# Where the weight sums of a seven-product feed forward are made: DVE adds in place instead of accumulating DMAs, and the relu stores issued by SP

## The chip, the cores and the metric

The kernel runs on 1 core of one Trainium2 chip. The metric is the device time of one execution, in microseconds (us). Before the change the median of 3 runs is 1975.8 us (1973.03 to 1976.18).

## The reference

The program is one decoder block on 1024 tokens of width 1024: an S5 state-space mixer beside dilated window attention, cross attention to 256 memory tokens, and a squared-relu feed forward, each closed by a layer norm. The change touches the feed forward alone:

```python
D_FF = 4 * D_MODEL            # 1024 -> 4096 -> 1024, all float32
ff = jnp.square(jax.nn.relu(h @ w_ff1[l] + b_ff1[l])) @ w_ff2[l] + b_ff2[l]
h = layer_norm(DEEPNORM_ALPHA * h + ff, ln3_g[l], ln3_b[l])
```

## The kernel before

Both matrix products of the feed forward are cut into 2x2 quadrants and multiplied with seven products instead of eight (the Winograd form of Strassen's scheme). The seven weight operands of a block come from its four quadrants 11, 12, 21, 22: "1" is 11, "2" is 21, "3" is 22, "5" is 11+12, "7" is 12+22, "6" is 11+12+22 and "4" is the sum of all four. Each operand is split into a high part and a rest (ACT makes the high part by a cast, DVE subtracts it), and a product is three rounds of float32r matmuls over four pieces of depth: 12 matmuls of 128x512.

*First product* (here: stage one; 16 blocks j of two times 128 hidden columns). `operand` (L1468) makes one operand: the cast on L1472, the subtraction on L1473, and then whatever the raw quadrants need next. The raw quadrants of two blocks (even and odd j) lie in buffers X, Y, Z, V; blocks of even j have theirs in the tiles `wraw`, those of odd j in free corners of the tile `hn` and in `sg`. Before the change, the sums are made by DMA: `add_in` (L1457) issues a DMA from the queue of POOL that adds its source to what lies in the destination. In every block X takes 12 on top of 11, Z takes 12 on top of 22, V is built as 11+12+22, and Y takes V. The plain loads for block j+2 go out on the queue of SP as soon as a buffer has been read for the last time. Six pairs of split buffers `whi`/`wlo`, each for two operands, hold the operands ahead of TensorE: a pair is filled when the pair six before it has been multiplied (`Stream`, L114; `slot` and `pump` issue the work).

The results of the seven products are combined by `f1_evac`, which DVE runs from PSUM: after "2" one addition (L1589), after "6" the five operations L1593, L1594, L397, L1599 and L1603, after "4" one (L1607). ACT then applies relu (L1572) and square (L1573). Four operations of POOL (L1609 to L1614) make the sums of the activations that the second product needs. All seven results of a block are stored to HBM, into `f_dr` (L1584): numbers 1, 2 and 4 by ACT's queue, 5, 6, 7 and 3 by SP's. Every engine and queue takes its instructions in the order in which the program wrote them down; nothing reorders them.

*Second product* (stage two; 4 blocks c of 1024 hidden rows, 7 products each, 4 token groups t per product). Its stationary operands are read back from `f_dr` through the same stream: SP loads (L145), ACT casts (L158), DVE subtracts (L159). Its weight quadrants are 1 MB each; `f2_weights` makes an operand two products ahead (cast L1544, subtraction L1545), and again `add_in` makes the sums from HBM. The first block's raw weights are loaded from POOL's queue (L1531), behind POOL's work of stage one. The residual input, saved in `h2_dr`, is brought back by four 1 MB loads on POOL's queue (L1809) at the start of stage two, and DVE adds products to it (L397, L1754).

The functions that the diff touches, and what calls them:

Of the kernel before, what the change touches and what calls it, by code (L numbers as in the profile page):

```python
# [58 lines left out]
def block_kernel(ctx, tc, I, out, dbg=None):  # L59
# [128 lines left out]
    W = Stream()  # L188
# [1271 lines left out]
    def f1_begin():  # L1460
        a, b = (win.tile([128, 1024], FT, name="wraw", tag="wraw", bufs=2) for _ in range(2))
        row = rows.tile([128, D], FT, name="row2", tag="row2", bufs=1)
        raws[0] = [half(a, 0), half(a, 1), half(b, 0), half(b, 1)]
        raws[1] = [half(row, 0), half(row, 1)]
        load(raws[0], 0, "11", "21", "22", "11")
        load(raws[1], 1, "11", "21")


    def operand(j, q, h, l):
        X, Y, Z, V = raws[j % 2] if len(raws[j % 2]) == 4 else raws[j % 2] + [None, None]  # L1470
        src = {"1": X, "2": Y, "3": Z, "4": Y, "5": X, "6": V, "7": Z}[q]
        act.copy(h, src)  # L1472
        dve.tensor_sub(l, src, h.bitcast(FT))  # L1473
        nxt = raws[(j + 1) % 2]
        if j == 0 and q in "12":
            add_in(V, w1(j, "12" if q == "1" else "22"))
        at = "57" if j == 1 else "15"
        if 0 < j < 15 and q in at:
            add_in(nxt[3], w1(j + 1, "12" if q == at[0] else "22"))
        if q == "1" and j != 1:  # L1480
            add_in(X, w1(j, "12"))
        elif q == "3":
            add_in(Z, w1(j, "12"))
# [10 lines left out]
        if j == 0 and q == "3":  # L1494
            add_in(Y, V)

# [17 lines left out]
    t_free = []  # L1514
    w2slot = []
    w2 = {}
# [10 lines left out]

    def w2_load(c, n, e=sp):
        if c < 4:
            w2[c, n] = w2slot.pop(0)  # L1530
            e.dma_start(w2[c, n], w2_src(c, n))  # L1531

    T2 = {}

    def f2_weights(n):
        if n >= len(f2_made):
            return
        c, q = f2_made[n]
        h, l = T2[c, q] = t_free.pop(0)
        X, Y, Z = (w2.get((c, i)) for i in ("11", "21", "22"))  # L1540
        if q == "6":
            add_in(Y, X)
        src = {"1": X, "2": Y, "3": Z, "4": Y, "5": X, "6": X, "7": Z}[q]
        act.copy(h, src)  # L1544
        dve.tensor_sub(l, src, h.bitcast(FT))  # L1545
        if q == "1":
            add_in(X, w2_src(c, "12"))
        elif q == "5":
            add_in(X, w2_src(c, "22"))
        elif q == "3":  # L1550
            add_in(Z, w2_src(c, "12"))
        elif q in "674":
            w2slot.append({"6": X, "7": Z, "4": Y}[q])
            if q != "4":
                w2_load(c + 1, "21" if q == "6" else "22")

# [22 lines left out]
    def f1_evac(j, q, p):  # L1579
# [102 lines left out]
    for n, (j, q) in enumerate(f1_seq):  # L1682
        p = bank()
        f1_product(j, q, p)
        f1_evac(j, q, p)
        if n == 1:
            W.cap = 10 ** 9
        slot()
        if j == 15:
            if q == "5":  # L1690
                wr = [actp.tile([128, 4, SEQ], FT, name="w2raw", tag=n) for n in ("acth0", "actl0")]
                w2slot += [a[:, :, 512 * i:512 * i + 512] for a in wr for i in range(2)]
# [229 lines left out]
```

## Time and profile before

| | |
|---|---|
| median of 3 runs | 1975.8 us |
| the profiled execution: its time, its span | 1979.96 us, 1978.2 us |
| TensorE busy / mean granted clock | 1832.2 us (93%) / 0.968 |
| DVE, ACT, POOL busy | 1188.8 (60%), 704.0 (36%), 760.4 (38%) us |
| moved by DMA | 273.43 MB, of it 50.86 MB on POOL's queue |
| stage one | about 1282 to 1596 us of the span |
| stage two | about 1596 to 1950 us, then 28 us of layer norm and stores |

A busy TensorE says little here, since a matmul that waits counts as idle only where nothing runs. Stage one holds 103 products after the first four half products, and stage two 112, each of 12 matmuls, so the time of a matmul in a stretch without waits, set against the time that the stretch took, tells what waiting costs. Two other things are to be read from such a page: which engine a waiting instruction names as its releaser, and who released that one. Here a chain of DVE and ACT, which wait for each other in turn, stands behind TensorE.

### The profile page before, as it was taken

The page shows a single profiled execution, that of the slowest core. Times are in us where ns is not written, and L with a number is a line of the kernel's source. Part 1 is how long each engine was busy: PE and PEld are TensorE (multiplying, and loading weights), DVE is VectorE, ACT ScalarE, POOL GpSimd, SP SyncE. Part 2 cuts the span into 40 slices and gives each one's busy share as a digit, 9 for nine tenths or more (in the row PEclk, how much of TensorE's full clock was granted, in tenths as well). Part 3 has the DMA queues.
Part 4 walks back from the last instruction along what each step waited for, and adds up shares of the span by engine and source line. Part 5 has one row for each costly group of instructions (what it writes and reads, how often), then busy time and mean ns, then how long its engine had stood idle before and what let it go on. Part 6 is the DMA issues. An engine that isn't in the chain of part 4 may idle for free. (4 is left out here: it accounts for less than half of the span.)

```text
span 1978.2 us, 24975 instructions
## 1 busy us (share of the span) xinstructions
PE 1832.2 (93%) x9112; PEld 1567.8 (79%) x9112; DVE 1188.8 (60%) x1994; ACT 704.0 (36%) x1176; POOL 760.4 (38%) x859
## 2 busy tenths in 40 slices
PE   7899999999999989999999999779999975999993
PEld 7798788899999977888887878658777754888872
DVE  6527736766665765344575466754555534765798
ACT  4333333332332435222124322434455443432421
POOL 3305696555556245222061023445455341001142
PEclk9999999999999999999999999899999987999997
DMA  6545561120211243424411133477778668889742
GB/s 253 179 119 193 184 195 44 57 73 25 86 34 35 83 138 102 136 90 137 177 47 43 54 115 103 108 190 197 193 209 216 183 198 245 247 207 208 221 119 85
DMA packets 138634, 273.43 MB, mean 138 GB/s; under 512 B 24720, under 2 KB 44304, under 8 KB 138512
## 3 DMA queue, kind: packets, MB, share of 16 engines
q1 hardware_dynamic: 100992, 195.28, 29.8%
q0 software_dynamic: 24560, 50.86, 13.8%
q10 hardware_dynamic: 12960, 25.70, 3.5%
q8 instruction: 72, 1.18, 0.2%
q14 instruction: 50, 0.41, 0.1%
HBM read 195.15 MB, written 68.26 MB: 133 GB/s over the span
## 5 line engine op out<-in xcount | busy, mean ns | idle before, releaser
L159 DVE TENSOR_TENSOR wlo<-wraw,whi 128x1024 fp32r<-128x1024 f32 (+1 forms) x171 | 217.6, 1279 | 224.5 <-ACT whi L158 223.8
L158 ACT CAST whi<-wraw 128x1024 fp32r<-128x1024 f32 (+1 forms) x171 | 170.7, 999 | 335.1 <-DMA wraw<-f_dr 159.7
L100 PE MATMUL mm<-whi,acth 128*128 128x512 f32 (+1 forms) x704 | 282.2, 401 | 0.0
L102 PE MATMUL mm<-whi,actl 128*128 128x512 f32 (+1 forms) x704 | 271.1, 385 | 0.0
L101 PE MATMUL mm<-wlo,acth 128*128 128x512 f32 (+1 forms) x704 | 270.9, 385 | 0.0
L100 PE MATMUL mm<-acth,whi 128*128 128x512 f32 (+1 forms) x640 | 248.5, 388 | 21.7 <-DVE hn L1593 8.4
L102 PE MATMUL mm<-acth,wlo 128*128 128x512 f32 (+1 forms) x640 | 245.7, 384 | 2.8 <-DVE wlo L159 2.5
L101 PE MATMUL mm<-actl,whi 128*128 128x512 f32 (+1 forms) x640 | 245.4, 383 | 0.3 <-DVE actl L279 0.3
L102 PEld LDWEIGHTS mm<-whi,actl 128*128 128x128 f32 x704 | 168.6, 239 | 15.4
L101 PEld LDWEIGHTS mm<-wlo,acth 128*128 128x128 f32 x704 | 169.1, 240 | 14.2
L100 PEld LDWEIGHTS mm<-whi,acth 128*128 128x128 f32 x704 | 168.1, 239 | 15.4
L100 PEld LDWEIGHTS mm<-acth,whi 128*128 128x128 f32 x640 | 124.1, 194 | 46.1 <-issue 14.6
L102 PEld LDWEIGHTS mm<-acth,wlo 128*128 128x128 f32 x640 | 123.4, 193 | 26.9 <-DVE wlo L159 3.0
L101 PEld LDWEIGHTS mm<-actl,whi 128*128 128x128 f32 x640 | 123.9, 194 | 22.1 <-DVE actl L279 0.5
L1473 DVE TENSOR_TENSOR wlo<-wraw,whi 128x512 fp32r<-128x512 f32 x56 | 53.2, 975 | 92.6 <-ACT whi L1472 92.6
L100 PE MATMUL ax<-acth,whi 128*128 128x512 f32 x232 | 93.7, 404 | 15.0 <-DVE hn L1593 10.5
L246 POOL TENSOR_TENSOR rs<-rs 128x2 f32<-128x2 f32 x30 | 18.4, 614 | 221.7 <-DVE rs L243 220.1
L101 PE MATMUL ax<-actl,whi 128*128 128x512 f32 x232 | 92.5, 399 | 3.2 <-DVE actl L1545 3.2
L102 PE MATMUL ax<-acth,wlo 128*128 128x512 f32 x232 | 92.5, 399 | 3.0 <-DVE wlo L159 3.0
L1458 POOL DMA_DIRECT2D w2raw<-in_wff_dram x12 | 14.6, 1216 | 201.5 <-DVE pl L1545 112.8
L1572 ACT ACTIVATE hn<-hn,cols 128x512 f32<-128x512 f32 x64 | 46.5, 727 | 117.3 <-DVE hn L397 52.2
L100 PE MATMUL ax<-ph,whi 128*128 128x512 f32 x164 | 65.3, 398 | 11.0 <-ACT ph L1544 11.0
(434 smaller groups left out, 4329.0 us busy)
## 6 DMA issues: line engine op xcount, KB each, us to landing
wraw<-f_dr SPq DMA_DIRECT2D x56, 512.0 KB
w2raw<-in_wff_dram POOLq DMA_DIRECT2D x15, 1024.0 KB, 10.5
f_dr<-hn SPq DMA_DIRECT2D x56, 256.0 KB
f_dr<-hn ACTq DMA_DIRECT2D x48, 256.0 KB
w2raw<-in_wff_dram SPq DMA_DIRECT2D x9, 1024.0 KB
wraw<-in_wg_dram SPq DMA_DIRECT2D x16, 512.0 KB
gl<-g_dr SPq DMA_DIRECT2D x32, 256.0 KB
wraw<-b_dr SPq DMA_DIRECT2D x16, 512.0 KB
```

Source lines behind the costliest of these rows:

```text
L100: pe.matmul(o, lhsT=lh, rhs=rh, start=first, stop=False)
L101: pe.matmul(o, lhsT=lh, rhs=rl, start=False, stop=False)
L102: pe.matmul(o, lhsT=ll, rhs=rh, start=False, stop=last)
L158: act.copy(h[:, :n], r[:, :n])
L159: dve.tensor_sub(l[:, :n], r[:, :n], h[:, :n].bitcast(FT))
L246: e.tensor_mul(t, z, z)
L1458: pool.dma_start(dst, src, accum_op=OP.add)
L1473: dve.tensor_sub(l, src, h.bitcast(FT))
L1572: act.activation(x, x, AF.Relu, bias=cols[:, COL_F1 + b:COL_F1 + b + 1], scale=1.0)
```

## The change

Stage one: the four quadrants are loaded plainly (V now takes 12) and DVE makes the sums in the buffers, right behind the subtraction that last needed the old content. Stage two: DVE makes 12+22 and 11+12+22; 11+12 (from block 1 on) and the sum of all four remain accumulating DMAs, but from one buffer on the chip to another. All seven stores of a block go out on SP's queue. The cap that held the filling of operands back in the first blocks is lifted earlier. The next block's quadrant 11 is loaded after operand "3" and not with product "1", the first block's 12 is loaded along with 21 and 11, and the gains of the last layer norm are loaded two products later.

```diff
@@ f1_begin
-        load(raws[0], 0, "11", "21", "22", "11")
+        load(raws[0], 0, "11", "21", "22", "12")
@@ operand
+        if (j, q) == (1, "5"):
+            dve.tensor_add(X, X, V)
+            dve.tensor_add(V, V, Z)
+            dve.tensor_add(Z, Z, X)
+        src = {"1": X, "2": Y, "3": Z, "4": Y, "5": X, "6": Z, "7": V}[q]
         act.copy(h, src)
         dve.tensor_sub(l, src, h.bitcast(FT))
-        nxt = raws[(j + 1) % 2]
-        if j == 0 and q in "12":
-            add_in(V, w1(j, "12" if q == "1" else "22"))
-        at = "57" if j == 1 else "15"
-        if 0 < j < 15 and q in at:
-            add_in(nxt[3], w1(j + 1, "12" if q == at[0] else "22"))
         if q == "1" and j != 1:
-            add_in(X, w1(j, "12"))
+            dve.tensor_add(X, X, V)
         elif q == "3":
-            add_in(Z, w1(j, "12"))
-        elif q == "2" and j > 1:
-            add_in(Y, V)
+            if j != 1:
+                dve.tensor_add(V, V, Z)
+                dve.tensor_add(Z, Z, X)
         elif q == "5":
             load([X], j + 2, "11")
         elif q == "6":
-            load([V], j + 2, "11")
+            dve.tensor_add(Y, Y, Z)
+            load([Z], j + 2, "22")
         elif q == "7":
-            load([Z], j + 2, "22")
+            load([V], j + 2, "12")
@@ f2_weights
-        if q == "6":
-            add_in(Y, X)
-        src = {"1": X, "2": Y, "3": Z, "4": Y, "5": X, "6": X, "7": Z}[q]
+        src = {"1": X, "2": Y, "3": Z, "4": Y, "5": X, "6": Z, "7": V}[q]
         act.copy(h, src)
         dve.tensor_sub(l, src, h.bitcast(FT))
-        if q == "1":
-            add_in(X, w2_src(c, "12"))
-        elif q == "5":
-            add_in(X, w2_src(c, "22"))
+        if n == 0:
+            dve.tensor_add(X, X, V)
+        elif q == "1":
+            add_in(X, V)
         elif q == "3":
-            add_in(Z, w2_src(c, "12"))
+            dve.tensor_add(V, V, Z)
+            dve.tensor_add(Z, Z, X)
+            add_in(Y, Z)
+            w2_load(c + 1, "11", X)
...
@@ f1_evac
-            (act if n in (1, 2, 4) else sp).dma_start(f_dr[n - 1, :, j, :], x)
+            sp.dma_start(f_dr[n - 1, :, j, :], x)
@@ first blocks of stage one
-    load(raws[1][3:], 1, "11")
-    add_in(raws[1][0], w1(1, "12"))
-    add_in(raws[1][3], w1(1, "12"))
-    add_in(raws[1][3], w1(1, "22"))
+    load(raws[1][3:], 1, "12")
...
-    add_in(raws[1][1], raws[1][3])
-    W.cap = W_FF + 6
+    W.cap = 10 ** 9
@@ end of stage one (j == 15, after product "5")
-                w2_load(0, "21", pool)
-                w2_load(0, "11", pool)
+                for i in (1, 0, 3):
+                    w2_load(0, ("11", "21", "22", "12")[i], w2slot[i], pool)
...
-    add_in(w2[0, "11"], w2_src(0, "12"))
-    w2_load(0, "22", pool)
+    w2_load(0, "22", w2slot[2], pool)
@@ stage two, loop over products
-                if (c, q) == (3, "1"):
+                if n == 23:
-                if q == "1" and c < 3:
-                    w2_load(c + 1, "11")
```

Lines of the changed kernel that stand in the rows below: L1477 is the subtraction of `operand`, L1479, L1482, L1483 and L1487 are the new additions, L1588 to L1606 are the operations of `f1_evac` (before: L1589 to L1607), L1583 is the store, L1527 the load of a quadrant of stage two.

On DVE, from the evacuation of product "2" of a block in stage one to the one after the next product "6", in the kernel before:

```order
L1589 TENSOR_TENSOR hn<-hn,ax 128x512
L1473 TENSOR_TENSOR wlo<-wraw,whi 128x512 x2
L1593 TENSOR_TENSOR hn<-mm,hn 128x512
L1594 TENSOR_TENSOR hn<-ax,hn 128x512
L397 SCALAR_TENSOR_TENSOR hn<-hn,mm 128x512
L1599 TENSOR_TENSOR hn<-hn,mm 128x512
L1603 TENSOR_TENSOR hn<-hn,mm 128x512
L1473 TENSOR_TENSOR wlo<-wraw,whi 128x512 x2
```

The same stretch in the changed kernel:

```order
L1588 TENSOR_TENSOR hn<-hn,ax 128x512
L1477 TENSOR_TENSOR wlo<-wraw,whi 128x512
L1479 TENSOR_TENSOR wraw<-wraw 128x512
L1477 TENSOR_TENSOR wlo<-wraw,whi 128x512
L1482 TENSOR_TENSOR wraw<-wraw 128x512
L1483 TENSOR_TENSOR wraw<-wraw 128x512
L1592 TENSOR_TENSOR hn<-mm,hn 128x512
L1593 TENSOR_TENSOR hn<-ax,hn 128x512
L397 SCALAR_TENSOR_TENSOR hn<-hn,mm 128x512
L1598 TENSOR_TENSOR hn<-hn,mm 128x512
L1602 TENSOR_TENSOR hn<-hn,mm 128x512
L1477 TENSOR_TENSOR wlo<-wraw,whi 128x512 x2
```

Three additions now stand in the queue ahead of the evacuation of product "6"; the order of the rest is the same.

On POOL, from the end of stage one into stage two, in the kernel before (L1614 is the last of the four sums of a block, L1458 an accumulating DMA, L1531 a weight load, L1809 a load of the residual):

```order
L1614 TENSOR_TENSOR sg<-hn 128x512
L1531 DMA w2raw<-in_wff_dram 128x4x512 x2
L1609 TENSOR_TENSOR hn<-hn 128x512
L1610 TENSOR_TENSOR hn<-hn 128x512
L1613 TENSOR_TENSOR hn<-hn 128x512
L1614 TENSOR_TENSOR hn<-hn 128x512
L1458 DMA w2raw<-in_wff_dram 128x4x512
L1531 DMA w2raw<-in_wff_dram 128x4x512
L1809 DMA hn<-h_dr 128x4x512 x2
L1458 DMA w2raw<-in_wff_dram 128x4x512
L1809 DMA hn<-h_dr 128x4x512
```

And in the changed kernel:

```order
L1613 TENSOR_TENSOR sg<-hn 128x512
L1527 DMA w2raw<-in_wff_dram 128x4x512 x3
L1608 TENSOR_TENSOR hn<-hn 128x512
L1609 TENSOR_TENSOR hn<-hn 128x512
L1612 TENSOR_TENSOR hn<-hn 128x512
L1613 TENSOR_TENSOR hn<-hn 128x512
L1527 DMA w2raw<-in_wff_dram 128x4x512
L1799 DMA hn<-h_dr 128x4x512 x3
L1458 DMA w2raw<-w2raw 128x4x512
L1799 DMA hn<-h_dr 128x4x512
```

The first accumulating DMA has become a plain load ahead of the last block's sums, and the third load of the residual no longer stands behind an accumulating DMA.

On SP, from the last stores of block 14 on, in the kernel before:

```order
L1584 DMA f_dr<-sg 128x512
L145 DMA wraw<-f_dr 128x1024 x3
L1584 DMA f_dr<-hn 128x512 x4
L145 DMA wraw<-f_dr 128x1024
L1531 DMA w2raw<-in_wff_dram 128x4x512
L145 DMA wraw<-f_dr 128x1024 x6
```

And in the changed kernel:

```order
L1583 DMA f_dr<-sg 128x512
L145 DMA wraw<-f_dr 128x1024
L1583 DMA f_dr<-hn 128x512
L145 DMA wraw<-f_dr 128x1024 x2
L1583 DMA f_dr<-hn 128x512 x6
L145 DMA wraw<-f_dr 128x1024 x7
L1527 DMA w2raw<-in_wff_dram 128x4x512 x2
```

The 1 MB load between the first and the second read-back after the stores has moved behind seven of them.

## Rows read from the trace of the kernel before

**Rows 1.** Stretches: span, busy PE, PEld, DVE, ACT, POOL, then PEclk, DMA share, GB/s.

```profile
1398.00:1560.00 162.00, 155.81 (x673) 127.56 (x674) 86.91 (x114) 79.42 (x128) 84.65 (x75) 0.98 0.79 203
1597.00:1668.00 71.00, 40.16 (x144) 30.64 (x144) 28.87 (x26) 23.35 (x24) 17.43 (x15) 0.79 0.74 234
1668.00:1895.00 227.00, 226.07 (x995) 186.84 (x994) 162.22 (x172) 84.22 (x66) 28.28 (x23) 1.00 0.88 225
```

**Rows 2.** Waits of PE, stage one, then 1596 to 1700 (us, times, longest).

```profile
PE ax L100 <- DVE hn L1593: 10.5, 6, 4.1
PE mm L100 <- DVE hn L1593: 9.9, 2, 8.4
...
PE ax L100 <- ACT ph L1544: 11.0, 1, 11.0
PE ax L101 <- DVE pl L1545: 10.6, 2, 7.4
```

**Rows 3.** DVE in order of time: start, us, work, idle before and its releaser.

```profile
1439.27 0.68 DVE L1593 TENSOR_TENSOR hn<-ax,hn 128x512 f32<-128x512 f32 x1
...
1447.97 1.74 DVE L1473 TENSOR_TENSOR wlo<-hn,whi 128x512 fp32r<-128x512 f32 x1 [4.64 <-ACT whi L1472]
...
1456.86 1.29 DVE L1473 TENSOR_TENSOR wlo<-wraw,whi 128x512 fp32r<-128x512 f32 x2 [2.53 <-ACT whi L1472]
...
1467.43 0.69 DVE L1473 TENSOR_TENSOR wlo<-wraw,whi 128x512 fp32r<-128x512 f32 x1 [2.21 <-ACT whi L1472]
...
1476.90 0.69 DVE L1473 TENSOR_TENSOR wlo<-wraw,whi 128x512 fp32r<-128x512 f32 x1 [2.54 <-ACT whi L1472]
...
1479.32 0.68 DVE L1593 TENSOR_TENSOR hn<-ax,hn 128x512 f32<-128x512 f32 x1
```

**Rows 4.** ACT in the same cycle.

```profile
1443.24 0.73 ACT L1572 ACTIVATE hn<-hn,cols 128x512 f32<-128x512 f32 x1 [0.40 <-ACT hn L1573]
...
1447.31 0.62 ACT L1472 CAST whi<-hn 128x512 fp32r<-128x512 f32 x1 [0.89 <-DMA hn<-in_wff_dram]
...
1466.78 0.63 ACT L1472 CAST whi<-wraw 128x512 fp32r<-128x512 f32 x1 [2.28 <-DMA wraw<-in_wff_dram]
```

**Rows 5.** DVE: an in-place subtraction alone; three subtractions beside POOL's sums.

```profile
1260.82 0.69 DVE L1384 TENSOR_TENSOR hn<-sg,hn 128x512 f32<-128x512 f32 x1
...
1566.81 4.78 DVE L1473 TENSOR_TENSOR wlo<-hn,whi 128x512 fp32r<-128x512 f32 x3 [3.64 <-ACT whi L1472]
```

**Rows 6.** ACT in the first blocks of stage one.

```profile
1307.03 0.62 ACT L1472 CAST whi<-wraw 128x512 fp32r<-128x512 f32 x1 [4.57 <-DMA wraw<-in_wff_dram]
...
1328.29 0.62 ACT L1472 CAST whi<-hn 128x512 fp32r<-128x512 f32 x1 [7.66 <-DMA hn<-in_wff_dram]
```

**Rows 7.** ACT, DVE, POOL and SP at the start of stage two, in this order.

```profile
1626.83 1.05 ACT L158 CAST whi<-wraw 128x1024 fp32r<-128x1024 f32 x1 [9.01 <-DMA wraw<-f_dr]
...
1638.86 1.05 ACT L158 CAST whi<-wraw 128x1024 fp32r<-128x1024 f32 x1 [10.49 <-DMA wraw<-f_dr]
1639.81 1.90 ACT L1544 CAST ph<-w2raw 128x2048 fp32r<-128x2048 f32 x1
...
1662.71 0.69 DVE L397 SCALAR_TENSOR_TENSOR hn<-hn,ax 128x512 f32<-128x512 f32 x1 [7.75 <-DMA hn<-h_dr]
1663.31 2.29 DVE L1545 TENSOR_TENSOR pl<-w2raw,ph 128x2048 fp32r<-128x2048 f32 x1
...
1621.70 1.24 POOL L1458 DMA_DIRECT2D w2raw<-in_wff_dram  x1
...
1645.95 1.24 POOL L1458 DMA_DIRECT2D w2raw<-in_wff_dram  x1 [18.95 <-DVE pl L1545]
1646.73 1.23 POOL L1809 DMA_DIRECT2D hn<-h_dr  x1
...
1622.20 0.38 SPq L145 DMA_DIRECT2D wraw<-f_dr  x1
1622.68 0.64 SPq L1531 DMA_DIRECT2D w2raw<-in_wff_dram  x1
```

More of the change, by code (lines that the diff above doesn't have):

```diff
@@ L1463, in f1_begin @@
         raws[0] = [half(a, 0), half(a, 1), half(b, 0), half(b, 1)]
-        raws[1] = [half(row, 0), half(row, 1)]
-        load(raws[0], 0, "11", "21", "22", "11")
+        raws[1] = [half(row, 0), half(row, 1), None, None]
+        load(raws[0], 0, "11", "21", "22", "12")
         load(raws[1], 1, "11", "21")
     def operand(j, q, h, l):
-        X, Y, Z, V = raws[j % 2] if len(raws[j % 2]) == 4 else raws[j % 2] + [None, None]
-        src = {"1": X, "2": Y, "3": Z, "4": Y, "5": X, "6": V, "7": Z}[q]
+        X, Y, Z, V = raws[j % 2]
+        if (j, q) == (1, "5"):
[3 more added lines that the diff above has]
+        src = {"1": X, "2": Y, "3": Z, "4": Y, "5": X, "6": Z, "7": V}[q]
         act.copy(h, src)
         dve.tensor_sub(l, src, h.bitcast(FT))
-        nxt = raws[(j + 1) % 2]
-        if j == 0 and q in "12":
-            add_in(V, w1(j, "12" if q == "1" else "22"))
-        at = "57" if j == 1 else "15"
-        if 0 < j < 15 and q in at:
-            add_in(nxt[3], w1(j + 1, "12" if q == at[0] else "22"))
         if q == "1" and j != 1:
-            add_in(X, w1(j, "12"))
+            dve.tensor_add(X, X, V)
         elif q == "3":
-            add_in(Z, w1(j, "12"))
-        elif q == "2" and j > 1:
-            add_in(Y, V)
+            if j != 1:
+                dve.tensor_add(V, V, Z)
+                dve.tensor_add(Z, Z, X)
         elif q == "5":
@@ L1488, in operand @@
         elif q == "6":
-            load([V], j + 2, "11")
+            dve.tensor_add(Y, Y, Z)
+            load([Z], j + 2, "22")
         elif q == "7":
-            load([Z], j + 2, "22")
+            load([V], j + 2, "12")
         elif q == "4":
             load([Y], j + 2, "21")
-        if j == 0 and q == "3":
-            add_in(Y, V)
     f1_order = "1325764"
@@ L1514, in block_kernel @@
     t_free = []
-    w2slot = []
     w2 = {}
@@ L1526, in w2_src, with w2_load @@
         return I["wff2"][c, ("11", "12", "21", "22").index(n)].rearrange("p (j c) -> p j c", j=4)
-    def w2_load(c, n, e=sp):
+    def w2_load(c, n, dst, e=sp):
         if c < 4:
-            w2[c, n] = w2slot.pop(0)
-            e.dma_start(w2[c, n], w2_src(c, n))
+            w2[c, n] = dst
+            e.dma_start(dst, w2_src(c, n))
     T2 = {}
@@ L1539, in f2_weights @@
         h, l = T2[c, q] = t_free.pop(0)
-        X, Y, Z = (w2.get((c, i)) for i in ("11", "21", "22"))
-        if q == "6":
-            add_in(Y, X)
-        src = {"1": X, "2": Y, "3": Z, "4": Y, "5": X, "6": X, "7": Z}[q]
+        X, Y, Z, V = (w2.get((c, i)) for i in ("11", "21", "22", "12"))
+        src = {"1": X, "2": Y, "3": Z, "4": Y, "5": X, "6": Z, "7": V}[q]
         act.copy(h, src)
         dve.tensor_sub(l, src, h.bitcast(FT))
-        if q == "1":
-            add_in(X, w2_src(c, "12"))
-        elif q == "5":
-            add_in(X, w2_src(c, "22"))
+        if n == 0:
+            dve.tensor_add(X, X, V)
+        elif q == "1":
+            add_in(X, V)
         elif q == "3":
-            add_in(Z, w2_src(c, "12"))
[L1552 to L1555, printed above, removed]
+            dve.tensor_add(V, V, Z)
+            dve.tensor_add(Z, Z, X)
+            add_in(Y, Z)
+            w2_load(c + 1, "11", X)
+        elif q == "6":
+            w2_load(c + 1, "22", Z)
+        elif q == "7":
+            w2_load(c + 1, "12", V)
+        elif q == "4":
+            w2_load(c + 1, "21", Y)
     nat_gemm(Cat(ph, xh), Cat(pl, xl), evac_xo, (range(4), range(4, 8)), True)
@@ L1685, in block_kernel @@
         f1_evac(j, q, p)
-        if n == 1:
-            W.cap = 10 ** 9
         slot()
@@ L1691, in block_kernel @@
                 wr = [actp.tile([128, 4, SEQ], FT, name="w2raw", tag=n) for n in ("acth0", "actl0")]
-                w2slot += [a[:, :, 512 * i:512 * i + 512] for a in wr for i in range(2)]
-                w2_load(0, "21", pool)
-                w2_load(0, "11", pool)
+                w2slot = [a[:, :, 512 * i:512 * i + 512] for a in wr for i in range(2)]
+                for i in (1, 0, 3):
+                    w2_load(0, ("11", "21", "22", "12")[i], w2slot[i], pool)
             elif q in "6724":
                 t_free.append(A7[q])
-    add_in(w2[0, "11"], w2_src(0, "12"))
-    w2_load(0, "22", pool)
+    w2_load(0, "22", w2slot[2], pool)
     f2_weights(0)
```

## The prediction

> **What bounds the kernel now.** I read the busy time by stretch first, then who waits for whom on TensorE, then the order of time on DVE and ACT. Only the feed forward is touched, so the stretches from 1282 us on count.
>
> In the middle of stage two, 995 matmuls take 227 us with TensorE busy throughout: 0.228 us each [rows 1]. That is the price without waits. In stage one 673 matmuls take 162 us, 0.2407 us each [rows 1]. Two blocks are 14 products of 12 matmuls: 168 x 0.2407 = 40.4 us, where TensorE alone would need 168 x 0.2272 (busy time over count, same row) = 38.2 us. So stage one is not bound by TensorE, though that is 96% busy. It waits there for L1593, the first operation that DVE runs after product "6", 20.4 us in all [rows 2]. The start of stage two is worse: 144 matmuls in 71 us, at a granted clock of 0.79 [rows 1], with waits for the weight operands [rows 2]. In these 71 us some 38 are lost (71 - 144 x 0.228).
>
> Why is DVE late in stage one? Follow one cycle of two blocks, from one L1593 to the second next: 1439.27 to 1479.32, 40.05 us [rows 3]. Each idle time of DVE shown in it ends with a cast of ACT. And ACT's casts stand in its queue behind relu and square, which wait for DVE. So the two engines hand work to and fro, one after the other, and this chain, not their busy time (86.9 and 79.4 of 162 us, rows 1), sets the pace. Some of the handing over is waiting for accumulated weights: ACT sits 0.89 and 2.28 us until such a DMA has landed [rows 4].
>
> **Stage one, the steady cycle.** All of this is counted along the chain.
>
> Removed: the two DMA waits of ACT, 0.89 + 2.28 = 3.2 us [rows 4], and 0.2 us for a third that DVE shows hardly at all. Six stores per cycle leave ACT's queue. Between a square and the next relu with a store between them 0.40 us pass [rows 4]; all six lie between an evacuation by DVE and the casts that DVE waits for, so 6 x 0.40 = 2.4, and the casts behind them gain another 0.4. Sum: 6.2 us.
>
> Added: eight additions of 128x512 per cycle. Six stand between L1588 and L1592, where POOL is done: an in-place operation of two SBUF operands takes 0.69 us alone [rows 5], and two such in a row 1.29 [rows 3], so 6 x 0.64 = 3.8. The two of Y and Z fall behind the evacuation of "4", where POOL makes its sums: three subtractions take 4.78 us beside POOL, 1.59 each [rows 5], so 2 x 1.59 = 3.2. And in every second block operand "4" can be cast only after that addition, one more trip over ACT: its cast is 0.62 [rows 4], partly hidden; with the drift of the POOL window I take 0.1. Sum: 7.1 us.
>
> Cycle after: 40.05 - 6.2 + 7.1 = 40.95 us. It is above the 38.2 of TensorE, so the chain stays the bound. Against the mean of 40.4 it costs 0.5 us per cycle, over the four cycles from 1398 to 1560 us, 2 us. Bounds: if the adds hid behind ACT, the cycle falls to TensorE's 38.2, at most 2.2 x 4 = 9 us gained there and some 3 in the stretches at its two ends; if all eight cost 1.59, it is 40.05 - 6.2 + 12.8 = 46.7, which I don't believe, since POOL works only about 6 us per block (84.65 us of 162, DMA issues included, rows 1).
>
> What the new adds wait for: the plain loads go out two blocks ahead, at the last reading of the buffer, so they have some 28 us. On SP they now stand behind the stores, some of which wait for POOL's sums; a store moved there is issued when ACT's square ends, and SP does nothing else but loads with that slack. I cost this at nothing; if a load came late it would cost what the two waits above cost now, 3.2 us per cycle.
>
> By the Trainium skill, "SBUF — State Buffer", section "Who interferes with whom", a DVE instruction with two SBUF inputs and a GpSimd instruction that reads SBUF exclude each other for the whole instruction. The trace agrees in kind, 1.59 against 0.69 us [rows 5]. By this rule an addition that starts just after one of POOL's would wait all of it and the cycle could be a further 1 us longer; the sum above goes by the row.
>
> **Stage one, first blocks.** ACT waits 4.57 and 7.66 us there for quadrants being accumulated [rows 6]. Both go: 12.2 us. In exchange the sums of blocks 1, 2 and 3 (9 additions between the evacuations of blocks 0 and 2, about half beside POOL: 5 x 0.64 + 4 x 1.59 = 9.6) come before the evacuation of product "6" of block 2; two stores less on ACT return 0.8. Gain 3.4, of which one addition earlier (operand "6" of block 0, in front of the last evacuations of cross attention, beside POOL, 1.6) gives 1.6 back: 2 us. Bounds: 12 gained (all adds hidden) to 5 lost (all adds at 1.59, and a wait stays). Stage one in all: 2 - 2 = 0 from the sums; at its end six stores less on ACT in the last two blocks give some 2. I take 2 us gained, between 14 gained and 12 lost.
>
> **Start of stage two.** Here the queues change most. Call S the moment when the last stores of stage one are out (1622.2, when SP goes on, rows 7).
>
> Before: SP issues one read-back, then the 1 MB load of the next block's 11 at 1622.68, then the next read-backs [rows 7]. POOL's queue at the same time holds the accumulation of 12 (1621.70), 22, and two loads of the residual. The second read-back lands at 1638.8 = S + 16.6; ACT stands 10.49 us for it, with the cast of operand "5" behind it, which ends the 11.0 us wait of TensorE [rows 7, 2]. Then the third residual load goes out only at 1646.73, because the accumulation in front of it waits 18.95 us for DVE; it lands at 1662.7, and DVE is stuck for 7.75 us in front of operand "3" [rows 7], the larger part of the 10.6 us in the last row of [rows 2].
>
> After: no 1 MB load stands between the read-backs, the accumulation of 12 is gone (12 came earlier, DVE adds it), and the three residual loads follow each other. The first read-back took from S to 1626.83, 4.6 us; a second one right behind it should land near S + 9, and with the two casts (1.05 and 1.90, rows 7) TensorE gets "5" at about S + 12 and not S + 19.5 (1641.7): 7.5 us less. On POOL's queue 22 and three residual loads are 4 MB. Before, the same queue moved 6 MB from 1621.70 to 1662.7 (two accumulations, 22 and three residual loads), 6.8 us per MB; at that rate the third residual load lands at S + 27, by 6 to 8 us per MB between S + 24 and S + 32, and not S + 40.5. Operand "3" follows some 3 us later (0.69 + 2.29, rows 7). So TensorE is there 8 to 16 us earlier. I take 12, and 1 us for ACT's stores of block 15; against it DVE's addition of X (a 2048-column operation, 2.29 us, rows 7) stands behind operand "2" and waits for 12 to have landed; it lies beside POOL's last sums and before the evacuations, and costs 1 us of the gain. The two sums of block 0 (4.6 us) follow operand "3" and lie under its four groups on TensorE, 48 x 0.228 = 10.9 us. Net 12 us gained. Bounds: 22 gained (both waits of rows 2 gone) to 3 lost (the loads bound as before and X's addition is added).
>
> **Rest of stage two.** TensorE is busy 226.07 of 227 us [rows 1]; six DVE operations of 2.29 us come in, two per block of 28 x 12 x 0.228 = 76 us. DVE is busy 162 of 227 [rows 1] and TensorE has eight banks, so I cost this at nothing; without that cover it would be 4.6 us once or twice. The layer norm at the end is the same.
>
> **Sum.** 2 + 12 = 14, with the lower clock at 0.79 returning about 1 us over a shorter gap: 15 us. The profiled execution took 1979.96 us (span 1978.2 and 1.8 around it), so it would be 1965. The median of the runs is 4.2 us lower, 1975.8, and the same 15 us off it give **1961 us**.
>
> **Rivals.**
>
> *The chain gets longer (slower).* The place is the DVE-ACT chain of stage one. For it: each addition stands in order in front of an evacuation that TensorE waits for, and rows 5 show that two-operand work more than doubles beside POOL. If all adds of a cycle, and the subtractions next to them, run beside POOL more often than I counted, a cycle reaches 43.5 us: 3.1 x 6 cycles = 19 us lost, 12 gained later, about 1982 us. It decides from a cycle of 42.6 on. Against it: POOL's sums end before the six adds start. The skill's rule above (same page and section) speaks for this rival, the measured 1.59 against it being dearer.
>
> *The start of stage two is bound by transfers anyway (no gain).* The 12 that left this place goes out with the first two weight loads instead, as a third MB beside the first read-backs, so those come later, and X's addition waits for it. Then 12 becomes 0 to 4: about 1973 us. Against it: at 0.74 DMA share the stretch has room [rows 1]. The skill's "DMA: Bandwidth & Descriptors", section "Queues, rings and completion order", says that an engine takes turns between queues; by that a third MB on POOL's queue would leave SP's read-backs their half. No run here shows it.
>
> *TensorE becomes the bound (faster still).* If additions fall into DVE's idle times, stage one gains 12 more: about 1948 us. For it: DVE is busy 87 of 162 us. Against it: its idle times all end with ACT.
>
> **Chances.** Forecast 0.54 (own range 1953 to 1969), slower chain 0.16, no gain 0.17, TensorE bound 0.13. Within 0.2% (4 us) a measurement of this kernel can't tell a change from none. Faster by more: 0.54 + 0.13 + a third of 0.17 = 0.72; the same: most of the rest of 0.17 and a little of the slower chain, 0.13; slower: 0.15. The range reaches from 1946 to 1978.
>
> **What the new profile would show.** Right: no ACT wait for `in_wff` in stage one, cycles between second next L1592 of 40 to 42 us, DVE idle before L1477 still ended by ACT, TensorE still waiting for L1592 by 2 to 3 us per cycle, the 11.0 us wait for L1538 below 5 us, and the third residual load issued within 3 us of the second. Wrong: cycles at 38.2 or above 42.6; ACT waiting for read-backs for 10 us as before; new TensorE waits after 1668 us.

## The result, and the profile after

The changed kernel takes 1956.97 us (median of 4 runs, 1955.03 to 1957.64) against 1975.99 us for the kernel before beside it: ratio 0.9905, 95% interval 0.9888 to 0.9922. It is 19 us faster; 1961 was forecast.

The profiled execution took 1956.8 us, 23 us less than the one before; that one lay 4 us above its median, so the two traces together show some 4 us too much. Both pages, busy time first, begin so. Before:

```profile
PE 1832.2 (93%) x9112; PEld 1567.8 (79%) x9112; DVE 1188.8 (60%) x1994; ACT 704.0 (36%) x1176; POOL 760.4 (38%) x859
```

After:

```profile
PE 1827.3 (93%) x9112; PEld 1563.5 (80%) x9112; DVE 1277.3 (65%) x2067; ACT 697.0 (36%) x1176; POOL 684.1 (35%) x771
```

DVE has 88 us more to do, and the kernel is still faster: shares of the span decide nothing here. The stretches, in the columns of [rows 1], are stage one and the rest of stage two after, then the first 60 us from S, before and after. S is again the moment when the last stores of stage one are out (1622.20 us before, 1617.37 after):

```profile
1398.00:1540.00 142.00, 132.68 (x577) 107.58 (x576) 101.63 (x124) 62.95 (x107) 42.80 (x27) 1.00 0.41 141
1645.00:1872.00 227.00, 225.89 (x995) 186.81 (x996) 187.88 (x182) 87.91 (x69) 22.57 (x17) 1.00 0.76 208
...
1622.00:1682.00 60.00, 38.42 (x153) 30.56 (x152) 25.16 (x25) 16.92 (x13) 8.47 (x9) 0.83 0.88 241
1617.00:1677.00 60.00, 53.30 (x222) 42.91 (x222) 39.47 (x34) 22.22 (x19) 5.96 (x7) 0.94 0.81 274
```

In stage one a matmul takes 0.246 us (142 over 577) where it took 0.241: a little worse, although the DMA share fell from 0.79 to 0.41. In the 60 us from S 222 matmuls are done where 153 were: 69 x 0.228 = 15.7 us, most of the gain. The rest is as before. TensorE's waits in stage one, then at the start of stage two, answer [rows 2] (L1592 is the L1593 of before, L1538 and L1539 the L1544 and L1545; L100, L101 and L102 are the three rounds of a product):

```profile
PE mm L100 <- DVE hn L1592: 11.1, 7, 5.3
PE ax L100 <- DVE hn L1592: 8.7, 5, 1.8
...
PE ax L100 <- ACT ph L1538: 4.4, 1, 4.4
PE ax L101 <- DVE pl L1539: 2.3, 2, 1.5
```

The wait for evacuations is still 20 us; that for operands "5" and "3" fell from 21.6 to 6.7 us. DVE in one cycle of stage one after, against [rows 3]:

```profile
1431.78 0.68 DVE L1592 TENSOR_TENSOR hn<-ax,hn 128x512 f32<-128x512 f32 x1
...
1443.18 1.77 DVE L1487 TENSOR_TENSOR sg<-sg,hn 128x512 f32<-128x512 f32 x1
...
1448.89 0.69 DVE L1477 TENSOR_TENSOR wlo<-wraw,whi 128x512 fp32r<-128x512 f32 x1 [1.96 <-ACT whi L1476]
1449.62 0.69 DVE L1479 TENSOR_TENSOR wraw<-wraw 128x512 f32<-128x512 f32 x1
...
1450.83 0.69 DVE L1482 TENSOR_TENSOR wraw<-wraw 128x512 f32<-128x512 f32 x1
1451.55 0.69 DVE L1483 TENSOR_TENSOR wraw<-wraw 128x512 f32<-128x512 f32 x1
...
1473.23 0.68 DVE L1592 TENSOR_TENSOR hn<-ax,hn 128x512 f32<-128x512 f32 x1
```

The cycle is 1473.23 - 1431.78 = 41.45 us. The three additions (L1479, L1482, L1483) stand in front of L1592; the addition of Y and Z (L1487) runs beside POOL and takes 1.77 us. And ACT, in front of the cast that this addition holds up:

```profile
1444.98 0.62 ACT L1476 CAST whi<-sg 128x512 fp32r<-128x512 f32 x1 [5.02 <-DVE sg L1487]
```

So ACT's waits for DMA have become waits for DVE. Over stage one they were, before (22.6 and 20.2 us for accumulated quadrants) and after:

```profile
ACT whi L1472 <- DMA wraw<-in_wff_dram: 22.6, 7, 4.8
ACT whi L1472 <- DMA hn<-in_wff_dram: 20.2, 12, 7.7
```

```profile
ACT whi L1476 <- DVE sg L1487: 36.9, 8, 5.0
```

The start of stage two after, SP, ACT, POOL, then TensorE, against [rows 7]; the last stores are out at S = 1617.37 us:

```profile
1617.37 24.58 SPq L145 DMA_DIRECT2D wraw<-f_dr  x7
...
1623.85 1.05 ACT L158 CAST whi<-wraw 128x1024 fp32r<-128x1024 f32 x1 [11.93 <-DMA wraw<-f_dr]
1626.43 1.04 ACT L158 CAST whi<-wraw 128x1024 fp32r<-128x1024 f32 x1 [1.05 <-DMA wraw<-f_dr]
1627.38 1.89 ACT L1538 CAST ph<-w2raw 128x2048 fp32r<-128x2048 f32 x1
...
1619.57 2.24 POOL L1799 DMA_DIRECT2D hn<-h_dr  x3 [1.93 <-DMA f_dr<-hn]
...
1629.33 0.80 PE L100 MATMUL ax<-ph,whi 128*128 128x512 f32 x1 [4.40 <-ACT ph L1538]
1645.65 0.50 PE L101 MATMUL ax<-pl,whi 128*128 128x512 f32 x1 [0.77 <-DVE pl L1539]
```

The second read-back comes 2.6 us behind the first, not 12; the residual loads go out together; TensorE has the rest of operand "3" at S + 28.3, where it came at S + 43.4.

### The profile page after: what moved, and what is told of

It is laid out like the page before. It is cut to its first block, busy times and chain, and to the rows that moved or that the text cites. A ratio compares the mean times of both kernels' runs of the same rounds, so it can differ in the third digit from the quotient of the medians.

```text
span 1954.6 us, 24829 instructions
## 1 busy us (share of the span) xinstructions
PE 1827.3 (93%) x9112; PEld 1563.5 (80%) x9112; DVE 1277.3 (65%) x2067; ACT 697.0 (36%) x1176; POOL 684.1 (35%) x771
## 5 line engine op out<-in xcount | busy, mean ns | idle before, releaser
L100 PE MATMUL mm<-whi,acth 128*128 128x512 f32 (+1 forms) x704 | 281.6, 400 | 0.0
L100 PE MATMUL mm<-acth,whi 128*128 128x512 f32 (+1 forms) x640 | 249.6, 390 | 24.8 <-DVE hn L1592 10.4
L102 PE MATMUL mm<-whi,actl 128*128 128x512 f32 (+1 forms) x704 | 270.7, 385 | 0.0
L101 PE MATMUL mm<-wlo,acth 128*128 128x512 f32 (+1 forms) x704 | 270.4, 384 | 0.0
L102 PE MATMUL mm<-acth,wlo 128*128 128x512 f32 (+1 forms) x640 | 246.0, 384 | 2.8 <-DVE wlo L159 2.6
L101 PE MATMUL mm<-actl,whi 128*128 128x512 f32 (+1 forms) x640 | 245.8, 384 | 0.3 <-DVE actl L279 0.3
L102 PEld LDWEIGHTS mm<-whi,actl 128*128 128x128 f32 x704 | 168.0, 239 | 15.3
L101 PEld LDWEIGHTS mm<-wlo,acth 128*128 128x128 f32 x704 | 168.6, 239 | 14.3
L100 PEld LDWEIGHTS mm<-whi,acth 128*128 128x128 f32 x704 | 167.5, 238 | 15.4
L100 PEld LDWEIGHTS mm<-acth,whi 128*128 128x128 f32 x640 | 124.4, 194 | 51.2 <-DVE hn L1592 12.9
L102 PEld LDWEIGHTS mm<-acth,wlo 128*128 128x128 f32 x640 | 123.6, 193 | 26.6 <-DVE wlo L159 3.0
L101 PEld LDWEIGHTS mm<-actl,whi 128*128 128x128 f32 x640 | 124.4, 194 | 22.2 <-DVE actl L279 0.5
L1608 POOL TENSOR_TENSOR hn<-hn 128x512 f32<-128x512 f32 x16 | 20.7, 1293 | 246.6 <-ACT hn L1572 246.6
L100 PE MATMUL ax<-acth,whi 128*128 128x512 f32 x232 | 92.4, 398 | 11.6 <-DVE hn L1592 8.7
L102 PE MATMUL ax<-acth,wlo 128*128 128x512 f32 x232 | 91.6, 395 | 3.0 <-DVE wlo L159 3.0
L101 PE MATMUL ax<-actl,whi 128*128 128x512 f32 x232 | 92.0, 396 | 2.6 <-DVE actl L1539 2.6
L1477 DVE TENSOR_TENSOR wlo<-wraw,whi 128x512 fp32r<-128x512 f32 x56 | 49.9, 916 | 56.5 <-ACT whi L1476 56.5
L100 PE MATMUL mm<-yh,whi 128*128 128x512 f32 x192 | 74.8, 390 | 0.7 <-ACT yh L1133 0.7
```

What stands on the lines that cost most here:

```text
L100: pe.matmul(o, lhsT=lh, rhs=rh, start=first, stop=False)
L101: pe.matmul(o, lhsT=lh, rhs=rl, start=False, stop=False)
L102: pe.matmul(o, lhsT=ll, rhs=rh, start=False, stop=last)
L1608: pool.tensor_sub(s1, x22, x21)
```

## The experiments

All times are medians; each ratio is to runs of the kernel before made on the same chip beside it. Single profiles of the same code up to the end of stage one reach it up to 9 us apart, so I read stage two from S to the end of the span. The code shown is an extract of each edit.

**One half of the change at a time.** Stage one alone: the changed kernel, with the loads, accumulations and slots of the second product as before.

```
@@ f2_weights, w2_load and their calls as before
-        if n == 0:
-            dve.tensor_add(X, X, V)
-        elif q == "1":
-            add_in(X, V)
+        if q == "1":
+            add_in(X, w2_src(c, "12"))
```

> The changed stage one (sums by DVE, stores on SP's queue) with the second product of the feed forward as it was before. Theory: the gain lies at the start of stage two; stage one gives some 5 us, so about 1971 us (1966 to 1975), and the waits of 10 us for a read-back and 7 us for the third residual load are there as before. Rival: the accumulating DMAs of stage one were the cost; then most of the 19 us is here, 1958 to 1962.

Measured: 1973.78 us, ratio 0.9999 (0.9988 to 1.0009). The long waits of stage two are there:

```profile
PE ax L100 <- ACT ph L1541: 10.0, 1, 10.0
PE ax L101 <- DVE pl L1542: 9.2, 2, 6.2
```

The rival falls. Stage one gives nothing that these runs can tell from zero, less than the 5 us that I read from the two traces. Its cycle is 1472.62 - 1431.17 = 41.45 us, as in the changed kernel.

Stage two alone is the counterpart, the changed kernel with stage one as before:

```
@@ operand, f1_evac and the first blocks as before
         if q == "1" and j != 1:
-            dve.tensor_add(X, X, V)
+            add_in(X, w1(j, "12"))
```

> Stage one as before, the second product of the feed forward as in the changed kernel. Theory: 14 us of the 19 come from here, so about 1962 us (1958 to 1966); TensorE's wait for operand 5 falls from 11 us to under 6, and DVE no longer waits 7 us for the residual. Rival (the gain is stage one's): 1970 to 1976. If the parts are independent, the two gains of this kernel and the one with stage one alone add up to 19 us.

Measured: 1957.25 us, ratio 0.9912 (0.9899 to 0.9925): 17.4 us of the 19. The theory holds, with a little more than its 14. The two halves add up to 17.6 of 18.8 us, within their intervals.

**What stage one paid for.** The stores back on ACT:

```
-            sp.dma_start(f_dr[n - 1, :, j, :], x)
+            (act if n in (1, 2, 4) else sp).dma_start(f_dr[n - 1, :, j, :], x)
```

> The changed kernel, with the stores of the three relu results of a block issued by ACT again. Theory: six issues of 0.40 us per cycle stand in the chain between DVE and ACT, and the cycle grows from 41.45 us by 2.4 to 2.8: over some 7 cycles 17 to 20 us slower than the changed kernel, about 1975 us. Rival: ACT has idle time beside them, the additions on DVE are what the chain waits for, and the time stays at 1957 to 1961.

Measured: 1978.69 us, ratio 1.0026 (1.0016 to 1.0035), so 22 to 24 us above the changed kernel (by medians, by ratios). DVE's first evacuation of "6", two blocks apart:

```profile
1440.08 0.69 DVE L1592 TENSOR_TENSOR hn<-ax,hn 128x512 f32<-128x512 f32 x1
...
1484.63 0.68 DVE L1592 TENSOR_TENSOR hn<-ax,hn 128x512 f32<-128x512 f32 x1
```

44.55 us, 3.1 more; 2.4 to 2.8 was expected. Six issues of 0.33 us, with no data moved by ACT, lengthen every cycle, because they stand between an evacuation and the casts.

The additions left out, so that the kernel lacks the weight sums of stage one:

> The changed kernel without the additions of weights in stage one: the products 5, 6, 7 and 4 there use the plain quadrants, so the weight sums are left out of the computation; loads, casts and everything else stay. Theory: the additions stand in the chain that TensorE waits for; without them the cycle of two blocks falls from 41.45 us to TensorE's 38.2, seven cycles give 20 us: about 1938 us (1934 to 1943). Rival: the additions lie in idle time of DVE and the cycle is set by the handing over of evacuations and casts alone: 1953 to 1957.

Measured: 1921.12 us, ratio 0.9733 (0.9720 to 0.9746). The theory's direction holds, its size doesn't: 34 to 36 us (by ratios, by medians), not 20. TensorE in the middle of stage one is then busy throughout, 628 matmuls at 0.226 us:

```profile
1398.00:1540.00 142.00, 142.00 (x628) 117.61 (x627) 86.24 (x103) 69.53 (x116) 45.00 (x30) 1.00 0.42 149
```

Measured at L1592 (here L1581) of blocks 0, 2 and 14: from the first to the second it takes 38.8 us where the changed kernel takes 49.7 (11 us, which I had not counted), from the second to the third 223.8 against 248.3 (24.5 us).

**The same additions at another place.** In the changed kernel DVE idles 2.0 to 2.6 us for ACT behind the evacuations of "6" and "4". The additions are collected there:

```
+        f1_sums(m)          # X+=V, V+=Z, Z+=X in front of the pair (2,5) or (5,7);
+                            # Y+=Z in front of (7,6) or (5,7)
         for i in range(2):
             operand(*f1_ops[2 * m + i], half(h, i), half(l, i))
```

> The changed kernel with the same additions in stage one, put at another place of DVE's order: none between the evacuations of products 2 and 6 any more; the three (four in odd blocks) come right after the evacuation of 6, in front of the operands 2 and 5 (5 and 7 in odd blocks), and Y and Z of even blocks in front of operands 7 and 6. There DVE idles 2.0 to 2.6 us for ACT in the changed kernel. Theory: what costs is not the work of the additions but that they stand in front of an evacuation that TensorE waits for; the cycle falls from 41.45 us to about TensorE's 38.1, and the time to 1930 us (1922 to 1942), near the kernel without sums (1921). Rival: DVE's time itself is short, or the additions now delay ACT's casts as much as before the evacuations: cycle 40.5 to 42, 1950 to 1960 us.

Measured: 1926.84 us, ratio 0.9777 (0.9763 to 0.9792), 25 to 30 us (by ratios, by medians) faster than the changed kernel with the same arithmetic. DVE at the place of the first row of the cycle above:

```profile
1415.59 0.69 DVE L1593 TENSOR_TENSOR hn<-ax,hn 128x512 f32<-128x512 f32 x1 [1.06 <-PE ax L102]
...
1418.97 0.68 DVE L1607 TENSOR_TENSOR hn<-hn,mm 128x512 f32<-128x512 f32 x1
1419.57 0.69 DVE L1494 TENSOR_TENSOR hn<-hn 128x512 f32<-128x512 f32 x1
...
1453.67 0.69 DVE L1593 TENSOR_TENSOR hn<-ax,hn 128x512 f32<-128x512 f32 x1 [1.06 <-PE ax L102]
```

The roles are reversed: DVE now waits for TensorE's product, the additions (from L1494) stand behind the evacuations, and the cycle is 1453.67 - 1415.59 = 38.08 us, TensorE's own. What cost was where the additions stood, not their work; DVE is even busier:

```profile
1398.00:1540.00 142.00, 142.00 (x629) 117.59 (x628) 108.65 (x138) 73.68 (x124) 47.64 (x31) 1.00 0.40 141
```

Which of the additions? Only Y and Z moved, from block 2 on:

```
@@ f1_fill; in operand the addition behind "6" stays for j < 2 only
+            if j > 1 and q == "57"[1 - j % 2]:     # q: first operand of the pair
+                dve.tensor_add(Y, Y, Z)
             for i in range(2):
                 operand(*f1_ops[2 * m + i], half(h, i), half(l, i))
```

> The changed kernel with one of the four additions of a block moved, from block 2 on: Y and Z no longer behind operand 6, beside POOL's sums and in front of the cast of operand 4, but ahead of operand 7 (even) or 5 (odd blocks). The three others stay in front of the evacuation of 6. Theory: on the chain this addition costs its 1.78 us twice per cycle and gives most of it back; cycle 39.0 to 40.0, about 1942 us (1937 to 1950). Rival: the chain only runs over the three in front of the evacuation; cycle 41.4, 1955 to 1959.

Measured: 1937.93 us, ratio 0.9809 (0.9794 to 0.9824), cycle 38.4 us (1365.33 to 1403.71). The time is in the theory's range, the cycle below what either expected: one addition of four, twice per cycle, gives 3.1 us of it back. And only the other three moved:

```
@@ f1_fill; in operand the three stay for j == 0 only
+            if j > 1 and q == "25"[j % 2]:
+                dve.tensor_add(X, X, V)
+                dve.tensor_add(V, V, Z)
+                dve.tensor_add(Z, Z, X)
```

> The changed kernel with the other three additions of a block moved, from block 2 on: behind the evacuation of 6, in front of operand 2 (even) or 5 (odd blocks). Y and Z stays where it is, behind operand 6 and beside POOL. Theory: the six additions of a cycle, 3.8 us of DVE, leave the chain and it falls under TensorE's 38.1; cycle 38.1 to 38.6, about 1934 us (1930 to 1940). Rival: the addition of Y and Z with its one more trip over ACT is the expensive part; cycle above 40, 1945 to 1957.

Measured: 1930.70 us, ratio 0.9775 (0.9761 to 0.9788), TensorE busy 142 of 142 us. The rival falls, and the cycle on DVE is shorter than the theory had it, 1476.82 - 1439.46 = 37.36 us:

```profile
1439.46 0.68 DVE L1598 TENSOR_TENSOR hn<-mm,hn 128x512 f32<-128x512 f32 x1
...
1476.82 0.69 DVE L1598 TENSOR_TENSOR hn<-mm,hn 128x512 f32<-128x512 f32 x1
```

That is below TensorE's 38.08 us: DVE started behind TensorE and catches up with it, and each of its waits is one for ACT. So this is the cycle of the chain itself. With all additions left out DVE catches up as well, from block 2 to block 4 in 34.28 us:

```profile
1315.04 0.69 DVE L1581 TENSOR_TENSOR hn<-mm,hn 128x512 f32<-128x512 f32 x1
...
1349.32 0.68 DVE L1581 TENSOR_TENSOR hn<-mm,hn 128x512 f32<-128x512 f32 x1
```

On the chain the prices add up: above these 34.28 us, Y and Z alone cost 3.1 us, the three others alone 4.1 (38.38), all four 7.2 (41.45). In the time the gains do not add up, since below 38.08 us TensorE limits. The chain with all additions was only 3.4 us above that; either group moved alone brings it below, or within 0.3 us.

Last, block 0 mended:

```
+        if (j, q) == (0, "4"):
+            dve.tensor_add(Y, Y, Z)
+            load([Z], 2, "22")
```

> The kernel with all sums in DVE's gaps (1926.8 us), with block 0 mended: there its four additions stand in front of the last evacuations of cross attention, and TensorE waits 11.1 us for one of these (7.3 in the changed kernel, 5.6 before). Here three of them go back to where the changed kernel has them and the last one goes behind these evacuations, in front of operand 4 of block 0. Theory: the wait falls to 5 to 6 us, 3 to 5 us faster, about 1922 to 1924 us. Rival: the wait moves to the next evacuation, no change: 1926 to 1928.

Measured: 1927.70 us, ratio 0.9759 (0.9744 to 0.9773). The wait fell as expected, from 11.1 to 5.6 us:

```profile
PE mm L100 <- DVE hn L1415: 5.6, 1, 5.6
PE ax L1367 <- DVE actl L279: 4.6, 1, 4.6
```

but the second row, the next wait, grew from 1.5 to 4.6 us: it moved, as the rival had it. The intervals of this kernel and of the one above overlap, so whether this edit gains anything is open. Both beat the kernel before by 2.2 to 2.4% and the changed kernel by 1.3 to 1.5%.

**What stage two gained by.** Three edits of the kernel before. The third residual load earlier:

```
-    hn_load = {0: ((0, 0), (0, 1)), 1: ((4, 1),), 2: ((4, 0),)}
+    hn_load = {0: ((0, 0), (0, 1), (4, 1)), 2: ((4, 0),)}
```

> The kernel before with one edit: the third residual load of the second product is issued with the first two, ahead of the accumulating DMA of 22 onto 11, instead of behind it. Theory: it stood 19 us behind an accumulation that waits for DVE; DVE's wait of 7.4 us in front of operand 3 goes, the 11 us wait for operand 5 stays: 4 to 7 us faster than before, about 1970 us. Rival: the transfers themselves bind (more megabytes ahead of the accumulation delay that one as much): 1973 to 1977.

Measured: 1967.89 us, ratio 0.9980 (0.9969 to 0.9991): 3.9 us, just under the 4 to 7 of the theory. DVE's wait in front of "3" is gone, and the wait for "5" is 9.9 us.

The 1 MB load later:

```
                 if q == "1" and c < 3:
-                    w2_load(c + 1, "11")
+                    w2[c + 1, "11"] = w2slot.pop(0)
+                if q == "5" and c < 3:
+                    sp.dma_start(w2[c + 1, "11"], w2_src(c + 1, "11"))
```

> The kernel before with one edit: the 1 MB load of the next block's 11 is issued on SP's queue two products later, so it no longer stands between the first and the second read-back. Theory: the second read-back lands some 9 us after the last stores and not 16.6; TensorE's wait of 11 us for operand 5 falls to 3 to 5 us, and the accumulation and the third residual load behind it move with it: 5 to 8 us faster, about 1968 us. Rival: the read-backs share the DMA engines with POOL's accumulations and loads, and come as late without that load: 1973 to 1977.

Measured: 1972.40 us, ratio 0.9998 (0.9988 to 1.0007). My theory failed in its end, not in its beginning. The second read-back did come early and the wait for the cast of "5" fell from 11.0 to 3.4 us, but then another wait stood there. TensorE, then DVE:

```profile
1628.13 0.50 PE L100 MATMUL ax<-ph,whi 128*128 128x512 f32 x1 [3.40 <-ACT ph L1544]
1637.19 0.79 PE L101 MATMUL ax<-pl,whi 128*128 128x512 f32 x1 [8.55 <-DVE pl L1545]
...
1634.24 0.69 DVE L397 SCALAR_TENSOR_TENSOR hn<-hn,ax 128x512 f32<-128x512 f32 x1 [7.97 <-DMA hn<-h_dr]
```

The subtraction for "5" (L1545) stands on DVE behind an evacuation that needs the second residual load, and that load stands on POOL's queue behind the accumulation of 12. In the kernel before this wait was hidden under the longer one: there its remainder was 1.6 us.

Both edits together:

> The kernel before with both edits: the third residual load early, the 1 MB load of the next 11 late; every weight sum still by an accumulating DMA. Theory: the order of these two loads is nearly all that the changed second product gained (17.7 us when it was tried alone): 13 to 18 us faster, 1957 to 1962 us. Rival: the sum of 12 by DVE and its early plain load are needed too: 5 to 9 us faster only.

Measured: 1965.30 us, ratio 0.9963 (0.9950 to 0.9976): 7.3 us, the rival's number. DVE's wait for the residual in front of "5" is 8.3 us. So this accumulation was taken out, and with it one weight sum of the computation:

```
-    add_in(w2[0, "11"], w2_src(0, "12"))
```

> The kernel before with the two moved loads of the second product, and the accumulating DMA of the first block's 12 onto 11 left out (that one weight sum is missing from the computation). Theory: what still holds the second product up there (DVE waits 8.3 us for the second residual load in front of operand 5) is that this accumulation lies ahead of that load on POOL's queue, where accumulating moves 130 to 210 GB/s and a plain load 390; without it the wait falls below 2 us and the time to 1957 to 1960 us, as with the whole changed second product. Rival: the wait belongs to the residual loads themselves (3 MB beside the read-backs); it stays, 1963 to 1967 us.

Measured: 1966.94 us, ratio 0.9949 (0.9933 to 0.9966). The wait went, and TensorE has the rest of "5" at S + 14.3 (S = 1620.94), as in the changed kernel (1631.65 - 1617.37). TensorE, then ACT:

```profile
1635.27 0.80 PE L101 MATMUL ax<-pl,whi 128*128 128x512 f32 x1 [1.82 <-DVE pl L1545]
...
1650.19 0.50 PE L100 MATMUL ax<-ph,whi 128*128 128x512 f32 x1 [2.45 <-ACT ph L1544]
1653.64 0.80 PE L101 MATMUL ax<-pl,whi 128*128 128x512 f32 x1 [2.96 <-DVE pl L1545]
...
1647.29 1.05 ACT L158 CAST whi<-wraw 128x1024 fp32r<-128x1024 f32 x1 [6.65 <-DMA wraw<-f_dr]
```

But the time did not fall to 1957 us; it is in the rival's range, though for another reason. Operand "3" now waits, for a read-back that lands at 1647.3, after the accumulation of 22 was issued at 1635.5. From S to the end of the span:

```
                                    S        end      us
kernel before                       1622.2   1978.2   356.0
stage one alone                     1615.1   1971.8   356.7
1 MB load late                      1615.4   1969.0   353.6
residual load early                 1617.3   1965.4   348.1
both                                1612.9   1958.4   345.5
both, accumulation of 12 left out   1620.9   1965.5   344.6
stage two alone                     1619.4   1956.5   337.1
changed kernel                      1617.4   1954.6   337.2
sums in gaps                        1592.2   1929.5   337.3
```

The last three agree to 0.2 us. By these single traces the order of the two loads makes 10.5 of the 19 us between old and new, leaving out the accumulation of 12 adds 0.9, and 7.5 are left. The traces do not all come from one chip. By runs beside each other the three shares are 7.3 (4.7 to 9.9), 2.8 and 7.3 us, and the residual load moved alone gave 3.9 (1.8 to 6.1) where its trace shows 7.9. So a rest of some 7 us stands either way; how the others split does not.

The rest comes with 22 loaded plainly and added by DVE, and the same for the later blocks. Most of it lies in the first 60 us from S. The columns are those of [rows 1]; the first row is the kernel with the accumulation of 12 left out, the second stage two alone:

```profile
1621.00:1681.00 60.00, 49.95 (x198) 39.77 (x198) 30.79 (x29) 20.02 (x17) 6.99 (x8) 0.91 0.90 276
1619.00:1679.00 60.00, 53.79 (x224) 43.36 (x223) 39.49 (x34) 22.24 (x19) 5.80 (x7) 0.93 0.81 273
```

26 matmuls fewer, at 0.228 us each, are 5.9 of the 7.5 us. They are lost at operand "3" of the first block, where TensorE has the rest of it at 1653.64 - 1620.94 = S + 32.7 and not at S + 28.3 to 28.5, and to the clock behind that wait (0.61 and 0.70 granted from 1651 to 1661 us, 1.00 with stage two alone). That the accumulation of 22 delays the read-back for "3" fits this, but is not shown: no run took that accumulation out alone. That accumulations load the DMA engines more is shown below.

## Why the prediction was right

**Time.** 1957 us measured, 1961 forecast, by the mechanism it named: little in stage one, the gain at the start of stage two. The signs of being right came (of ACT's waits for `in_wff` one of 0.4 us is left). One sign of being wrong came too, by its letter: ACT still waits 11.93 us for a read-back. But that is the first one; the wait for the second, which held up operand "5", fell from 10.49 to 1.05 us.

**Steady cycle.** 40.95 us forecast, 41.45 measured. The added term was right: 7.1 us forecast, 7.2 by the kernels above. The stores, put at 2.4 and 0.4, were 3.1. What was too large is the term of ACT's removed waits for DMA: 40.05 + 7.2 - 3.1 - 41.45 leaves 2.7 us for them where 3.4 stood. In the prediction a sentence by the Trainium skill, "SBUF — State Buffer", section "Who interferes with whom", allowed a further 1 us for such pairs excluding each other; the trace agrees in kind (1.77 us beside POOL, 0.69 alone), but the further 1 us did not come. Against the kernel before (12 blocks, six executions with that stage one: 240.8 to 246.7 us; after 248.3) the cost is 2 to 8 us where 2 stood, for four cycles; there are six.

**First blocks.** 3.4 us gained, of which 1.6 given back, was forecast. TensorE's wait for the last evacuations of cross attention rose from 5.64 to 7.28 us, the 1.6; but the wait behind it fell from 4.46 to 3.41, so only some 0.6 was given back. From the first to the third L1592 it took 52.7 to 54.4 us with the old stage one and 49.7 after, so some 4 were gained.

**Stage one in all** was put at 2 us between 14 gained and 12 lost; alone it measured 0.2 us gained, with an interval from 2.4 gained to 1.8 lost. That it came out near nothing is partly luck: the cycles lost more than the 2 us, and the first blocks gave more than the 2 us left of their gain. ACT's 42.8 us of waits for accumulated weights vanished, and no time was won in all, as DVE's additions in front of the evacuations took their place.

**Start of stage two** was the mis-sized term: "I take 12", with bounds of 22 and -3, and 1 for the clock. It measured 17.4 alone. The steps were close: "5" forecast at S + 12, measured at 1629.33 - 1617.37 = S + 12.0; "3" some 3 us behind a third residual load at S + 27, measured at S + 28.3 against S + 43.4 before. That is 15 us earlier, the upper end of the 8 to 16 from which I took 12. The sum counted the order of SP's and POOL's loads and the accumulation of 12, and these gave 10.1 us (6.7 to 13.2) when tried together. The other 7 us, which came with the accumulation of 22 and the later ones gone, were not in it: there it was short.

X's addition was to cost 1 us. It takes 3.36 us beside POOL's last sums, of which the last takes 3.33 us where it took 2.26: that is the 1 us, on the last store's path. The rest of stage two cost nothing, as said.

**Rivals.** The longer chain stayed below its 42.6. "Transfer-bound" fell: the first read-back did land later, at S + 6.5 and not S + 4.6, but the second followed at S + 9. With the 1 MB load alone moved the first one came at 1619.86 - 1615.40 = S + 4.5, so what delays it is not the order on SP. By the Trainium skill, "DMA: Bandwidth & Descriptors", section "Queues, rings and completion order", an engine takes turns between queues; the later first read-back beside POOL's plain loads agrees with that in kind, but no run separates it. "TensorE becomes the bound" did not happen here, but the kernels with moved additions are that rival, at 1927 to 1938 us where it was put at 1948. The additions needed another place. And 9 us from four cycles and 3 beside them had been counted, while the kernel with the sums in gaps takes 225.7 us from block 2 to block 14 (248.3 in the changed kernel) and 43.7 from block 0 to block 2 (49.7).

## What to carry to other kernels

In a chain where two in-order engines hand work to and fro, an operation's price is what stands behind it: the same additions cost 34 to 36 us in front of evacuations that the bound engine waits for, and 6 to 9 behind them. Before moving a DMA's work to an engine, find the idle times of that engine and put the work there in its order, not where the data happens to be at hand. When a long wait is removed, list what was hidden under it: here a load that came 8 us late stood under an 11 us wait, and removing the one alone gave nothing.

## What the runs showed of the hardware

An accumulating DMA took twice the DMA engines' time of a plain one here. In the kernel before, 1400 to 1540 us (queue, packets, MB, share of 16 engines; q0 holds POOL's accumulations, q1 SP's plain loads and stores):

```profile
q0 software_dynamic: 5040, 9.18, 39.6%
q1 hardware_dynamic: 8062, 14.68, 30.4%
```

4.3% per MB against 2.1%. In the changed kernel, where q0 is empty, it is 2.1% again:

```profile
q1 hardware_dynamic: 10755, 19.61, 40.6%
```

POOL's queue itself is not what costs. From 1619 to 1631 us of the changed kernel it moves plain loads only:

```profile
q0 software_dynamic: 831, 3.22, 70.9%
```

70.9% of 12 us for 3.22 MB is 2.6 us of all engines per MB; the accumulations took 6.0 (39.6% of 140 us, 9.18 MB).

TensorE's clock fell with its long pauses here. After the 11 us wait of the kernel before, the granted clock is 0.50, the 1.2 GHz level, while matmuls run again, and after the 7.4 us wait 20 us later it falls once more:

```profile
1642.00:1647.00 5.00, 1.85 (x4) 1.15 (x5) 4.24 (x4) 1.01 (x2) 1.05 (x2) 0.50 0.79 302
1662.00:1667.00 5.00, 1.35 (x3) 1.16 (x4) 4.29 (x3) 1.07 (x2) 1.10 (x2) 0.53 0.00 1
```

A matmul takes 0.45 us there (1.35 over 3), where it takes 0.226 in stretches at 1.00. In the changed kernel one such fall is left of the two, after the 4.4 us wait:

```profile
1631.00:1637.00 6.00, 5.35 (x14) 4.24 (x15) 3.02 (x4) 2.09 (x2) 0.00 (x0) 0.58 0.83 297
```
